# Two gate tiles moved behind the recurrence, two ahead of the sparse attention; the last expert pair summed in PSUM with the norm by halves

## Chip, cores and metric

The kernel runs on one core of a Trainium2 chip. The metric is the device time of one execution in microseconds (us). A core has TensorE (PE: matmuls, with its weight loads as PEld), VectorE (DVE), ScalarE (ACT), GpSimd (POOL) and SyncE (SP, which here issues most DMAs), each with its own instruction queue that is worked off in order. Engines wait for each other through semaphores.

## What is computed

Two blocks on 512 tokens of width 1024, all in float32. The first block has a recurrent branch, a sparse attention branch, two gates that mix them, and a mixture of 32 experts; its output goes through two norms into two layers of a second block. The lines that the change touches, cut from the reference:

```
xr, gr, q, ckv, qi, ki, wi, mg = jnp.split(u @ w_in[l], split_pts, axis=-1)
hr = rg_lru(causal_dwconv(xr, ...), ...)                       # recurrence, 1280 wide
y_a = (jax.nn.gelu(gr) * hr) @ w_rnn_out[l]
att = dsa_attention(q, rmsnorm(ckv, ...), qi, ki, wi, ...)     # top-128 keys of each query, 8 heads
y_b = att @ w_att_out[l]
ga, gb = jnp.split(jax.nn.sigmoid(mg), 2, axis=-1)             # two gates, 1024 wide each
mix = (ga * y_a + gb * y_b) @ w_out[l]
...
h = h + g2 * hier_moe(u2, ...)                                 # 32 experts, two per token
return rmsnorm(h, final_g)
# second block:
x = layer_norm(x, ln_in_g, ln_in_b)
for l in range(2): proj = x @ w_in[l]; ...
```

## The kernel before

A float32 product is made of three faster ones: each operand is split into a high part (`wh`, a cast on ScalarE, line 145) and a low part (`wl`, a subtraction on VectorE, line 146), and `mm3`/`mmk` (lines 300, 301, 303) add high times low, low times high and high times high in PSUM. So each weight piece costs ScalarE a cast, VectorE a subtraction, and TensorE three matmuls for each 128 rows. `FM.tile` makes one tile of 128 features by 512 tokens in this way: for an input of 1024 features 24 matmuls of 128x512, named `fm`. `TM` is the same with tokens in the rows; its `prepare` loads and splits the first pieces ahead of their use.

The kernel is written with a tile framework, which turns the program into one fixed queue of instructions for each engine. `weave` runs several generators beside each other and steps each in proportion to the weight given with it, so the weights set how their instructions interleave; `behind(a, b)` puts instruction a after b in that order without a semaphore.

`gate(d)` (line 677) makes one of 16 gate tiles: `fma.tile`, a sigmoid on ScalarE, a store to `gate_d` in HBM. Gates 0 to 7 are read again by `branch_a`, 8 to 15 by `branch_b`. In `rg_lru` (line 758) the recurrence goes through five groups of two blocks of 128 channels: `rg_first` (convolution), a gate tile, and, a group later, `rg_last` (the scan `hs`, a gelu gate `g2`, and its split `gT`). The group loop has a sixth pass that only runs the two last `rg_last`. Gates 0 to 9 are made there. It is woven with the index scores and the top-k selection (lines 638 and 639: maxima and replacements on VectorE). `branch_a` (line 784) then multiplies all ten `gT` with `w_rnn_out`, eight tiles of 30 matmuls.

In the sparse attention `att_score` (line 920) makes, for head h and query block i, the scores `as`, adds a bias (`bm`) and does a softmax (maximum `mx`, a sigmoid on ScalarE, reciprocal `su`); before head 0 it makes keys and values (`ak`, `av`) and the query tile of head 0, and at i = 3 the query tile of the next head. `att_out` transposes (`apt`) and splits (`pt`), `att_products` multiplies with the values (`ao`). It is woven, by `weave` on line 968, with `gate_b` (gates 10 to 15, weight 6) and `mod_rows` (vector-matrix products on VectorE, `macc`, with a short matmul `mrow`).

The experts run as 16 pairs. `pair_out` (line 1428) transposes the hidden rows (`hdt`, copied to `hp`), multiplies with the second weight (`e2`, both halves m of 512 columns in turns), and `outputs` (line 1297) scales to `y`, splits it (`yh`, `yl`), and `combine` adds the rows to the tokens: for each 128 tokens i and half m two matmuls with a 0/1 matrix `place` into PSUM (`cmb`), then a VectorE add to `h1[i][m]`. During one pair the `combine` of the pair before runs beside it. After the last pair (j = 15) the generator is emptied, then the loop at line 1964 norms each of four token tiles: squares on ScalarE with a sum (`ssq`), multiply by `final_g`, batch-norm statistics, and `norm` (line 1237), which ends in two halves of line 1240 and `turn`, the transposes `xt` and their splits `xT`. They feed `nav`, the first product of the second block, whose first three weight pieces are prepared (`nav_tm.prepare`) when the last pair is issued.

Of the kernel before, what the change touches and what calls it, by code (L numbers as in the profile page):

```python
# [64 lines left out]
def build(ctx, tc, I, out, dbg=None):  # L65
# [78 lines left out]
    def split(hi, lo, src, eng=None):  # L144
        S.copy(hi, src)  # L145
        (eng or V).tensor_tensor(lo, src, f(hi), OP.subtract)  # L146
# [234 lines left out]
    class TM:  # L381
# [25 lines left out]
        def piece(self, p, page=None):  # L407
# [7 lines left out]
            split(hi, lo, raw[:, k1:k1 + g1, :])  # L415
            return k0 + k1, g1, hi, lo

        def prepare(self):
            if self.first is None:
                self.first = [self.piece(p) for p in self.pieces[:self.lead]]  # L420
            return self
# [333 lines left out]
    def rg_lru():  # L755
        prev = []
        for g in range(6):
# [12 lines left out]
            if g < 5:  # L770
                prev = rg_decay(keep)
                yield

# [4 lines left out]
    weave((rg_lru(), 36), (chain(index_scores(), top_k(0, 6)), 44))  # L778
# [103 lines left out]
    def gate_b():  # L882
        for d in range(10, 16):
# [84 lines left out]
    weave((pipelined(8, att_score, att_out), 36), (gate_b(), 6), (mod_rows(0, 2, 1), 15))  # L968
# [262 lines left out]
    def normalizer(gvec, bvec, dst, paged=True):  # L1231
# [5 lines left out]
        def norm(i, v, mv, var, later=None):  # L1237
            r = rsqrt(var, 1, lambda: V.scalar_tensor_tensor(v, v, mv[:, 0:1], gR, OP.subtract, OP.mult))
            for cs in (slice(0, 512), slice(512, 1024)):
                V.scalar_tensor_tensor(v[:, cs], v[:, cs], r, bR[:, cs], OP.mult, OP.add)  # L1240
# [6 lines left out]
            else:  # L1247
                later.append(lambda: turn(i, v))

# [47 lines left out]
    def outputs(py, gtc, rows):  # L1297
# [12 lines left out]
        def combine():  # L1310
            after = yield
            for i in range(4):
                for m in range(2):
                    cs = slice(m * 512, m * 512 + 512)
                    ps = trp("cmb")
                    pl = place[:, i * 128:(i + 1) * 128]
                    mm = PE.matmul(ps, pl, yl[:, cs], start=True, stop=False)
                    if after is not None:
                        behind(mm, after)
                    PE.matmul(ps, pl, yh[:, cs], start=False, stop=True)  # L1320
# [108 lines left out]
    def pair_out(j, hd, ws):  # L1429
# [5 lines left out]
        S.copy(hp, b)  # L1435
        py = [mmp("e2") for _ in range(2)]
        for k in range(4):
            for m in range(2):
                cs = slice(m * 512, m * 512 + 512)
                both(py[m], hp[:, k * 128:k * 128 + 128], [w[:, cs] for w in ws[2 * k:2 * k + 2]], k == 0, k == 3)  # L1440
        return outputs(py, gt0[:, j:j + 1], rows0[:, :, j])
# [39 lines left out]
    for j in range(17):  # L1481
# [7 lines left out]
        if prev is not None:  # L1489
# [8 lines left out]
            if j == 16:  # L1498
                nav_tm.prepare()
        prev = hd  # L1500
    for _ in beside:
        pass
# [462 lines left out]
    for i in range(4):  # L1965
        a = h1t[i]

        ms = sm("ssq", 1)
        sq = pt_("sq", F32, (128, 1024))
        S.activation(sq, a, AF.Square, accum_out=ms)  # L1970
# [39 lines left out]
```

## Time and profile before

| | us |
|---|---|
| median of 3 runs | 3058.28 (3057.55 to 3060.16) |
| profiled execution | 3058.93, span 3057.2 |
| PE busy | 2893.9 (95%) |
| DVE busy | 1832.8 (60%) |
| ACT busy | 1137.3 (37%) |
| POOL busy | 196.3 (6%) |

Busy shares are means over stages with different limits. The mean granted TensorE clock is 0.987 of full speed. In the timeline rows a start time is in us from the start of the span, followed by the duration, and in brackets the idle time ahead of the instruction and what ended it. Instructions of one engine overlap a little, so the time from start to start is shorter than the duration shown.

### The profile page before, as it was taken

What the parts mean: (1) busy time and instruction counts of PE and PEld (TensorE: products, weight loads), DVE (VectorE), ACT (ScalarE), POOL (GpSimd) and SP (SyncE); (2) the same over time, 40 slices, a digit from 0 to 9 for tenths busy, and PEclk for the clock granted to TensorE, in tenths of its full rate; (3) what the DMA queues carried; (4) which work ended last, traced back from release to release, by engine and by line L of the source; (5) the groups of instructions that cost most, each with busy time, mean ns of one, the idle gap of its engine ahead of it and who ended that gap; (6) DMA issues with size and microseconds to landing.
All of it is one profiled execution on the core that took longest, in us unless ns stands there. A gap on an engine that the chain in (4) does not pass through costs nothing.

```text
span 3057.2 us, 36511 instructions
## 1 busy us (share of the span) xinstructions
PE 2893.9 (95%) x13749; PEld 2181.7 (71%) x13749; DVE 1832.8 (60%) x3549; ACT 1137.3 (37%) x1996; POOL 196.3 (6%) x216
## 2 busy tenths in 40 slices
PE   6999999889999979999999999999999989999998
PEld 5877777634333338888767888887888867788887
DVE  6899798733333265555888644436554689754434
ACT  4665244201000124444666322223443567332221
POOL 2000000100000001110002000000211000200000
PEclk9999999989999999999999999999999999999999
DMA  7333647789999964332335432424342234632342
GB/s 229 95 104 106 222 145 261 273 328 410 411 409 409 411 238 148 111 111 85 102 92 183 169 101 94 140 97 123 126 131 90 75 109 117 232 104 97 97 145 62
DMA packets 291648, 534.17 MB, mean 175 GB/s; under 512 B 29766, under 2 KB 172276, under 8 KB 287366
## 3 DMA queue, kind: packets, MB, share of 16 engines
q1 hardware_dynamic: 288872, 527.45, 49.4%
q0 software_dynamic: 2304, 4.20, 0.4%
q8 instruction: 110, 1.80, 0.3%
q14 instruction: 76, 0.62, 0.1%
q10 hardware_dynamic: 286, 0.09, 0.0%
HBM read 486.50 MB, written 44.38 MB: 174 GB/s over the span
## 4 chain that ended last, share of the span: by engine, by line
PE 56%; DMA 11%; DVE 6%; issue 3%; ACT 2%; POOL 1%; SPq 0%; DVEq 0%; POOLq 0%; ACTq 0%
PE fm L303 9%; PE fm L300 9%; PE fm L301 9%; DMA w<-in_moe_w_dram 7%; PE e L1391 4%; DMA w2r<-in_moe_w_dram 3%; PE ffo L303 2%; PE ffo L300 2%; PE ffo L301 2%; PE mix L300 1%; PE mix L301 1%; PE mix L303 1%; POOL tl L1666 1%; DVE wl L146 1%; DMA tl<-t_d 1%
## 5 line engine op out<-in xcount | busy, mean ns | idle before, releaser
L146 DVE TENSOR_TENSOR wl<-raw,wh 128x1024 fp32r<-128x1024 f32 (+3 forms) x403 | 461.7, 1147 | 307.9 <-ACT wh L145 306.3
L145 ACT CAST wh<-raw 128x1024 fp32r<-128x1024 f32 (+3 forms) x403 | 388.5, 966 | 550.0 <-PE fm L303 244.6
L300 PE MATMUL fm<-xT,wh 128*128 128x512 f32 (+1 forms) x1264 | 481.7, 384 | 0.0
L301 PE MATMUL fm<-xT,wl 128*128 128x512 f32 (+1 forms) x1264 | 479.5, 382 | 1.3 <-DVE wl L146 1.3
L303 PE MATMUL fm<-xT,wh 128*128 128x512 f32 (+1 forms) x1264 | 301.9, 381 | 0.0
L301 PEld LDWEIGHTS fm<-xT,wl 128*128 128x128 f32 x1264 | 238.3, 189 | 46.5 <-DVE wl L146 1.7
L300 PEld LDWEIGHTS fm<-xT,wh 128*128 128x128 f32 x1264 | 238.1, 188 | 45.0
L1391 PE MATMUL e<-w,xx 128*64 128x512 f32 x1024 | 257.1, 601 | 10.4 <-DMA w<-in_moe_w_dram 10.4
L303 PEld LDWEIGHTS fm<-xT,wh 128*128 128x128 f32 x1264 | 231.7, 188 | 45.5
L1391 PEld LDWEIGHTS e<-w,xx 128*64 128x64 f32 x1024 | 75.0, 137 | 157.7 <-issue 131.2
L1321 DVE TENSOR_TENSOR h<-h,cmb 128x512 f32<-128x512 f32 x128 | 80.7, 683 | 126.4 <-PE cmb L1320 126.2
L301 PE MATMUL fm<-uT,wl 128*128 128x512 f32 (+1 forms) x360 | 141.8, 394 | 2.7 <-DVE wl L146 2.6
L300 PE MATMUL fm<-uT,wh 128*128 128x512 f32 (+1 forms) x360 | 141.5, 395 | 0.0
L300 PE MATMUL ffo<-wl,hid 128*128 128x512 f32 x352 | 137.1, 390 | 0.0
L301 PE MATMUL ffo<-wh,hid 128*128 128x512 f32 x352 | 136.9, 389 | 0.0
L1391 PE MATMUL e<-w2r,hp 128*64 128x512 f32 x512 | 115.1, 596 | 10.1 <-ACT hp L1435 10.1
L1953 DVE SCALAR_TENSOR_TENSOR ffs<-ffs,fm 128x512 f32<-128x512 f32 x44 | 30.3, 688 | 137.7 <-ACT ffs L1952 137.7
L303 PE MATMUL ffo<-wh,hid 128*128 128x512 f32 x352 | 108.4, 389 | 0.0
L1955 DVE SCALAR_TENSOR_TENSOR ffs<-ffs,fm 128x512 f32<-128x512 f32 x44 | 30.2, 687 | 114.4 <-PE fm L303 114.4
L1952 ACT ACTIVATE ffs<-fm 128x512 f32<-128x512 f32 x44 | 26.3, 598 | 187.2 <-PE fm L303 187.2
L1391 PEld LDWEIGHTS e<-w2r,hp 128*64 128x64 f32 x512 | 41.1, 136 | 73.1 <-issue 58.3
L1307 DVE SCALAR_TENSOR_TENSOR y<-e,gts,g2R 128x512 f32<-128x512 f32 x32 | 22.9, 748 | 116.3 <-PE e L1391 116.0
(602 smaller groups left out, 5869.0 us busy)
## 6 DMA issues: line engine op xcount, KB each, us to landing
w<-in_moe_w_dram SPq DMA_DIRECT2D x192, 512.0 KB
raw<-in_w_in_dram SPq DMA_DIRECT2D x71, 1024.0 KB
w2r<-in_moe_w_dram SPq DMA_DIRECT2D x128, 512.0 KB
raw<-in_w_ffn_in_dram SPq DMA_DIRECT2D x44, 1024.0 KB
w<-in_moe_w_dram SPq DMA_DIRECT2D x32, 1024.0 KB
raw<-in_w_mod_dram SPq DMA_DIRECT2D x42, 512.0 KB
raw<-in_w_ffn_out_dram SPq DMA_DIRECT2D x20, 1024.0 KB
raw<-in_w_out_dram SPq DMA_DIRECT2D x12, 1024.0 KB
```

Of the source, the lines that this page charges most:

```text
L145: S.copy(hi, src)
L146: (eng or V).tensor_tensor(lo, src, f(hi), OP.subtract)
L300: PE.matmul(ps, l[0], r[1], start=start and n == 0, stop=False)
L301: PE.matmul(ps, l[1], r[0], start=False, stop=False)
L303: PE.matmul(ps, l[0], r[0], start=False, stop=stop and n == len(pairs) - 1)
L1307: V.scalar_tensor_tensor(y[:, cs], py[m], gtc, g2R[:, cs], OP.mult, OP.mult)
L1321: V.tensor_tensor(h1[i][m], h1[i][m], ps, OP.add)
L1391: mm = PE.matmul(ps[hs], lhs[:, hs], rhs[h], start=start, stop=stop)
L1666: G.tensor_tensor(th, m, th, OP.add)
L1952: S.activation(s, pgt, AF.Tanh, scale=0.5)
L1953: V.scalar_tensor_tensor(s, s, 1.0, pgt, OP.add, OP.mult)
L1955: V.scalar_tensor_tensor(s, s, 0.5, pup, OP.mult, OP.mult)
```

## The change

It has two parts. In the first, gates 10 and 11 are made at the end of `rg_lru`, after the last two `rg_last` (and the weave weight goes from 36 to 38); gates 12 and 13 are made ahead of the attention weave, and only 14 and 15 stay in it, with weight 2. In the second, for the last pair the products of `e2` run half by half, the table of the reciprocal square root is loaded on ScalarE right behind the copy `hp`, and the old rows `h1` are added by a matmul with the identity that opens each PSUM group, so `combine` hands over the PSUM tile and the VectorE add goes. The norm's squares and its multiply by `final_g` read that tile, half by half, in the order `LAST`; the statistics come by halves too. `nav_tm.prepare` runs inside the norm of token tile 0, its splits behind that tile's last operation.

```diff
         def prepare(self, after=None):
             if self.first is None:
-                self.first = [self.piece(p) for p in self.pieces[:self.lead]]
+                self.first = []
+                for p in self.pieces[:self.lead]:
+                    self.first.append(self.piece(p))
+                    if after is not None:
+                        behind(self.low, after)
...
             if g < 5:
                 prev = rg_decay(keep)
                 yield
+            else:
+                for d in (10, 11):
+                    gate(d)
+                    yield
...
-    weave((rg_lru(), 36), (chain(index_scores(), top_k(0, 6)), 44))
+    weave((rg_lru(), 38), (chain(index_scores(), top_k(0, 6)), 44))
...
     def gate_b():
-        for d in range(10, 16):
+        for d in range(12, 16):
...
-    weave((pipelined(8, att_score, att_out), 36), (gate_b(), 6), (mod_rows(0, 2, 1), 15))
+    gb = gate_b()
+    for _ in range(2):
+        next(gb)
+    weave((pipelined(8, att_score, att_out), 36), (gb, 2), (mod_rows(0, 2, 1), 15))
...
+    BANKS = [(i, m) for i in range(4) for m in range(2)]
+    LAST = [(0, 0), (1, 0), (0, 1), (1, 1)] + BANKS[4:]
...
         def combine():
             after = yield
-            for i in range(4):
-                for m in range(2):
+            for i, m in LAST if last else BANKS:
+                cs = slice(m * 512, m * 512 + 512)
+                ps = trp("cmb")
+                pl = place[:, i * 128:(i + 1) * 128]
+                if last:
+
+                    PE.matmul(ps, ident, h1[i][m], start=True, stop=False)
+                mm = PE.matmul(ps, pl, yl[:, cs], start=not last, stop=False)
...
+                PE.matmul(ps, pl, yh[:, cs], start=False, stop=True)
+                if last:
+                    after = yield ps
+                else:
                     V.tensor_tensor(h1[i][m], h1[i][m], ps, OP.add)
                     after = yield
...
+        steps = [(k, m) for k in range(4) for m in range(2)]
+        if j == 15:
+
+            steps.sort(key=lambda e: (e[1], e[0]))
+            behind(S.activation(const("table", [128, 1]), ones[:, 0:1], AF.Abs_reciprocal_sqrt), cast)
...
+    def norm_parts(i, m, ps):
+        a = h1[i][m]
+        if m == 0:
+            sts[i] = sm("ssq", 2), sm("bst", 12)
+        S.activation(sqs[i % 2][:, m * 512:m * 512 + 512], ps, AF.Square, accum_out=sts[i][0][:, m:m + 1])
+        V.tensor_tensor(a, ps, fgR[:, m * 512:m * 512 + 512], OP.mult)
+        bn_part(a, sts[i][1], m, 2)
+
+    def norm_in(i):
+        ms, st = sts[i]
+        v = sm("msq", 1)
+        V.tensor_scalar(v, ms[:, 0:1], ms[:, 1:2], 1e-6 * 1024, OP.add, OP.add)
+        mv = bn_done(st)
+        V.scalar_tensor_tensor(v, v, 1e-5 / 1024, mv[:, 1:2], OP.mult, OP.add)
+        return norm(i, h1t[i], mv, v)
+
+    sqs = [pt_("sq", F32, (128, 1024)) for _ in range(2)]
+    for n, (i, m) in enumerate(LAST):
+        norm_parts(i, m, beside.send(None))
+        if m:
+            last = norm_in(i)
+            if i == 0:
+                nav_tm.prepare(last)
...
-    for i in range(4):
-        a = h1t[i]
...
-        norm(i, a, mv, v)
```

How this moves instructions on the engines shows in three places. VectorE at the end of the recurrence, before (`g` and `gT` of the last two blocks, `m` and `selp` the top-k):

```order
429 L749 SCALAR_TENSOR_TENSOR g_442_2388<-g_442_2388,fm_2359 128x512
430 L747 SCALAR_TENSOR_TENSOR g_449_2435<-g_449_2435,fm_2406 128x512
431 L750 TENSOR_TENSOR g_442_2388<-g_442_2388,hs_2355 128x512
432 L639 MATCH_REPLACE selp_735<-m_459_2493,selp_735 128x256
433 L749 SCALAR_TENSOR_TENSOR g_449_2435<-g_449_2435,fm_2406 128x512
434 L146 TENSOR_TENSOR gT_2394<-g_442_2388,gT_2394 128x512
```

and now:

```order
428 L751 SCALAR_TENSOR_TENSOR g_447_2429<-g_447_2429,fm_2400 128x512
429 L754 TENSOR_TENSOR g_440_2382<-g_440_2382,hs_2349 128x512
430 L146 TENSOR_TENSOR wl_2480<-raw_2441,wh_2479 128x1024
431 L146 TENSOR_TENSOR gT_2388<-g_440_2382,gT_2388 128x512
432 L753 SCALAR_TENSOR_TENSOR g_447_2429<-g_447_2429,fm_2400 128x512
433 L146 TENSOR_TENSOR wl_2520<-raw_2514,wh_2519 128x640
```

The split `wl_2480` of gate 11 stands between the `g` of the last but one block and its `gT`; the two 128x640 splits of `branch_a`, which stood further ahead, come behind it. On TensorE at the same place, gate 11 is `fm_2478` and the first tile of `branch_a` is `fm_2518`; now:

```order
1115 L303 MATMUL fm_2443<-uT_398,wh_2444 128x512
1116 L300 MATMUL fm_2478<-uT_226,wh_2479 128x512
1117 L300 MATMUL fm_2518<-gT_1174,wh_2519 128x512
1118 L301 MATMUL fm_2478<-uT_226,wl_2480 128x512
1119 L300 MATMUL fm_2478<-uT_236,wh_2479 128x512
```

Before, `branch_a` began in row 1092, right behind the last tile of the recurrence; now gate 10 (`fm_2443`) and gate 11 stand between. TensorE at the scores of head 0, query block 3 (`as` with 128x512), before:

```order
1449 L303 MATMUL fm_3201<-uT_398,wh_3202 128x512
1450 L300 MATMUL as_3233<-kP_3034,qT_3110 128x512
1451 L301 MATMUL as_3233<-kP_3034,qT_3110 128x512
1452 L303 MATMUL as_3233<-kP_3034,qT_3110 128x512
1453 L300 MATMUL fm_3321<-uT_226,wh_3322 128x512
1454 L301 MATMUL fm_3321<-uT_226,wl_3323 128x512
```

and now:

```order
1545 L303 MATMUL fm_3333<-uT_398,wh_3334 128x512
1546 L300 MATMUL as_3365<-kP_3166,qT_3242 128x512
1547 L301 MATMUL as_3365<-kP_3166,qT_3242 128x512
1548 L303 MATMUL as_3365<-kP_3166,qT_3242 128x512
1549 L300 MATMUL as_3378<-kP_3176,qT_3362 128x128
1550 L959 MATMUL apt_3392<-ident,bm_3249 128x128 x2
```

Before, a gate tile (`fm_3321`, gate 11) and the query tile of head 2 followed these scores; now the first scores of head 1 and the transposes of head 0 follow at once, and gates 12 and 13 stand ahead of the keys instead. VectorE at the norms, from the end of token tile 1 to the first multiply of token tile 2, before:

```order
1563 L1240 SCALAR_TENSOR_TENSOR h_962_4959<-h_962_4959,rst_9674,lnb_9517 128x512 x2
1564 L146 TENSOR_TENSOR xT_9630<-xt_9645,xT_9630 128x128
1565 L1971 TENSOR_TENSOR h_963_4962<-h_963_4962,fgR_9513 128x1024
1566 L146 TENSOR_TENSOR xT_9631<-xt_9645,xT_9631 128x128
1567 L146 TENSOR_TENSOR xT_9624<-xt_9680,xT_9624 128x128
```

and now:

```order
1561 L1251 SCALAR_TENSOR_TENSOR h_962_4959<-h_962_4959,rst_9664,lnb_9517 128x512 x2
1562 L146 TENSOR_TENSOR xT_9602<-xt_9670,xT_9602 128x128
1563 L146 TENSOR_TENSOR xT_9603<-xt_9670,xT_9603 128x128
1564 L146 TENSOR_TENSOR xT_9606<-xt_9683,xT_9606 128x128
1565 L146 TENSOR_TENSOR xT_9604<-xt_9670,xT_9604 128x128
1566 L146 TENSOR_TENSOR xT_9607<-xt_9683,xT_9607 128x128
1567 L146 TENSOR_TENSOR xT_9605<-xt_9670,xT_9605 128x128
1568 L1530 TENSOR_TENSOR h_963_4962<-cmb_9697,fgR_9513 128x512
```

Six `xT` splits of the tile just finished stand ahead of the next tile's multiply, which stood ahead of them.

## Rows read from the trace of the kernel before

**Rows 1.** Windows: stretch, length; busy PE, PEld, DVE, ACT, POOL; clock, DMA share, GB/s.

```profile
260.00:280.00 20.00, 18.52 (x82) 14.91 (x80) 20.00 (x33) 15.76 (x24) 0.00 (x0) 1.00 0.15 47
282.00:290.00 8.00, 5.30 (x13) 3.77 (x14) 6.84 (x18) 1.97 (x4) 0.00 (x0) 0.57 0.53 149
386.00:496.00 110.00, 109.33 (x568) 87.76 (x567) 105.46 (x241) 53.96 (x120) 0.00 (x0) 0.99 0.51 174
380.00:500.00 120.00, 116.97 (x590) 92.27 (x590) 113.86 (x258) 58.77 (x129) 0.00 (x0) 0.97 0.50 169
1110.00:1147.00 37.00, 23.56 (x93) 15.76 (x91) 35.93 (x82) 14.75 (x40) 1.40 (x2) 0.82 0.22 80
```

**Rows 2.** Timeline of PE, `branch_a`: start, us, instruction, [idle before, what ended it].

```profile
273.34 0.39 PE L300 MATMUL fm<-gT,wh 128*128 128x512 f32 x1
...
278.83 0.50 PE L301 MATMUL fm<-gT,wl 128*128 128x512 f32 x1 [1.48 <-DVE wl L146]
...
283.67 0.79 PE L300 MATMUL fm<-gT,wh 128*128 128x512 f32 x1 [3.40 <-DVE gT L146]
...
285.92 0.80 PE L300 MATMUL fm<-gT,wh 128*128 128x512 f32 x1 [1.03 <-DVE gT L146]
...
336.64 0.27 PE L180 MATMUL rowst<-ident,rows 60*128 60x60 f32 x1
```

**Rows 3.** Timeline of DVE at the end of the recurrence.

```profile
263.54 1.22 DVE L146 TENSOR_TENSOR wl<-raw,wh 128x1024 fp32r<-128x1024 f32 x1
...
277.95 0.82 DVE L146 TENSOR_TENSOR wl<-raw,wh 128x640 fp32r<-128x640 f32 x1
278.69 1.22 DVE L743 TENSOR_TENSOR_SCAN hs<-ra,tx 128x512 f32<-128x512 f32 x1
...
281.33 0.69 DVE L750 TENSOR_TENSOR g<-g,hs 128x512 f32<-128x512 f32 x1
```

**Rows 4.** Waits of PE from 200 to 260: total, times, longest.

```profile
PE fm L301 <- DVE wl L146: 2.6, 3, 1.2
```

**Rows 5.** Timeline of PE, front of the attention (queries, gate 10, scores).

```profile
342.58 0.40 PE L300 MATMUL fm<-uT,wh 128*128 128x512 f32 x1
...
348.05 0.39 PE L300 MATMUL fm<-uT,wh 128*128 128x512 f32 x1
...
350.94 0.33 PE L301 MATMUL as<-kP,qT 128*128 128x128 f32 x1 [1.21 <-DVE nlam L866]
...
361.74 0.39 PE L300 MATMUL as<-kP,qT 128*128 128x512 f32 x1
```

**Rows 6.** Timeline of DVE, start of the softmax chain to the first `pt`.

```profile
367.98 0.29 DVE L860 TENSOR_TENSOR lp<-lv 128x128 f32<-128x128 f32 x1 [4.67 <-DMA lv<-in_diff_lambda_dram]
...
380.42 1.28 DVE L806 SCALAR_TENSOR_TENSOR macc<-raw,csil,macc 128x1024 f32<-128x1024 f32 x1
...
381.69 0.67 DVE L146 TENSOR_TENSOR pt<-apt,pt 128x512 fp32r<-128x512 f32 x1
```

**Rows 7.** Timeline of PE, last pair and norm.

```profile
1099.61 7.09 PE L1391 MATMUL e<-w2r,hp 128*64 128x512 f32 x32 [0.68 <-ACT hp L1435]
1108.15 0.50 PE L1317 MATMUL cmb<-yl,place 128*128 128x512 f32 x1 [1.45 <-DVE yl L146]
...
1124.10 1.97 PE L1257 MATMUL xt<-ident,h 128*128 128x128 f32 x8 [11.06 <-DVE h L1240]
```

**Rows 8.** One tile's instructions, `mrow`: durations in ns, first and last start.

```profile
L814 PE MATMUL mrow<-macc,ones x4: 590/592/592, 401.2 to 402.5; 128*1 128x512 f32 x4
```

**Rows 9.** Timeline of DVE, last adds, `nav` splits, first and last norm end.

```profile
1109.77 3.67 DVE L1321 TENSOR_TENSOR h<-h,cmb 128x512 f32<-128x512 f32 x6 [0.15 <-PE cmb L1320]
1113.36 2.35 DVE L146 TENSOR_TENSOR wl<-raw,wh 128x1024 fp32r<-128x1024 f32 x2
...
1123.30 1.41 DVE L1240 SCALAR_TENSOR_TENSOR h<-h,rst,lnb 128x512 f32<-128x512 f32 x2
...
1145.58 1.42 DVE L1240 SCALAR_TENSOR_TENSOR h<-h,rst,lnb 128x512 f32<-128x512 f32 x2
```

## Prediction before the run

> **What bounds the kernel now.** I read the page's busy shares first (TensorE fills the span, so only places where it waits or repeats work can move the end), then the windows, timelines and waits of the three stretches that the diff touches, and the chain of waits behind them. The first two stretches stand ahead of the experts' weight stream, which is released by the router and hence by what lies before it; the third stands behind it. So a gain or loss in each is carried to the end one for one.
>
> At the end of the recurrence VectorE has no gap: 20.00 of 20 us in 260 to 280 [rows 1]. TensorE is ahead of it: `branch_a` starts at 273.34, then waits 1.48, 3.40 and 1.03 us for the splits `wl`, `gT` and `gT`, and ends at 336.64 [rows 2]. Behind the long wait the granted clock is 0.57 of full speed in 282 to 290, a mean over the 1.2 and 2.4 GHz levels; TensorE is busy 5.30 us there with 13 matmuls [rows 1], which at 0.227 us apart (as ahead of the wait) take 2.95: some 2.1 to 2.3 us lost to the clock. The hole is thus 5.9 of waits and about 2.1 of slow clock.
>
> In the sparse attention both engines are nearly full: 386 to 496 has TensorE at 109.33 and VectorE at 105.46 of 110 us; 380 to 500 leaves VectorE 6.14 us idle [rows 1]. The start of the softmax chain is what the front has to reach: VectorE waits 4.67 us for the load `lv`, begins at 367.98, and splits the first `pt` at 381.69 [rows 6].
>
> In the last stretch VectorE is the bound: eight adds of the last pair, three splits of `nav` weights, then four norms; 35.93 busy of 37 us [rows 1, 9], while TensorE stands 11.06 us until the first `xt` [rows 7].
>
> **Part A1, gates 10 and 11 behind the recurrence.** One gate tile or query tile of 24 matmuls takes 5.47 us (342.58 to 348.05) [rows 5]; two bring 10.94 us of TensorE work ahead of `branch_a`, into a hole of 8.0. Filling all of it would cost 2.9 us. But the second gate needs its own `wl`, which is a VectorE operation of 1.22 us in the stream that is already full [rows 1, 3]. In the new order it stands behind `g2` times `hs` of the last but one block, which starts at 281.33 and frees VectorE at 281.93 [rows 3]. Up to there the new order has one `wl` of 1024 more (+1.13 issue to issue), two `wl` of 640 fewer (-0.74 each, the next starting at 278.69 after 277.95) and one top-k maximum fewer (about -0.4): VectorE arrives at 281.2, and `wl` is ready at 282.4. TensorE arrives sooner: VectorE has some 1.7 us less top-k work in front at the time of the first gate, and TensorE's 2.6 us of waits on `wl` between 200 and 260 [rows 4] can shrink by that, so gate 10 runs 271.6 to 277.1 and gate 11 stops after its first matmul and one of `branch_a`, at 277.4. It waits 5 us where before there was work, then has 23 matmuls (5.2) and 239 of `branch_a` (54.3) to go: 341.9 against 336.64, **+5.2**. The clock would be low behind that wait as it is now behind the 3.40 (2.1 lost), so I take **+7.3** for the end of `branch_a` (E). Ends: clock loss 0 to 3.4 (all of 282 to 289 at half speed), VectorE's lead 0.8 better or worse: +4.4 to +9.4. The `gT` splits, later by one `wl`, are covered by gate 11. Queued behind the new waits: on ScalarE the table load and gate 10's sigmoid stand ahead of the last `g2` tanh and both `gT` casts, which VectorE does not want before 283; on SP's queue the two gate stores stand ahead of a `w_rnn` load that is read two tiles, over 13 us, later. Both cost nothing unless the second gate ends after about 295.
>
> The Trainium skill, in "Perfetto Trace Analysis", section Optimization Strategies, says to keep the matmul engine as highly used as possible, and where it waits, to relieve the engines that block the path. The first half speaks for this move, the second against it, since the blocking engine gets two splits more; by the first alone A1 is the 2.9 of a filled hole (below as a rival), by the rows it is 7.3.
>
> **Part A2, gates 12 and 13 ahead of the attention, 10 and 11 gone from it.** Before, the front from E runs: keys and values to 342.58 (5.9), `q0` 5.47, then a gate mixed with scores and `q1` to 361.74 (13.7, of it 1.21 a wait for a small VectorE chain that now lies earlier) [rows 5]. The four scores of head 0 ended at E+25.8 and the chain then waited for `lv`, E+31.3. Now two gates (10.9) precede: 10.9 + 5.9 + 5.5 + 12.5 + 0.7 = E+35.5, plus 0.6 for `bm`: the chain starts at E+36.1, the load is long there. From its start to the first `pt` it took 13.7 us [rows 6]; in the new order one `macc` of 1.28 [rows 6] stands behind instead: 12.4, so first `pt` at E+48.5 against E+45.05 (381.69 less 336.64): **+3.4**. After that TensorE has 10.9 us less to do, but VectorE's work to the last `att` shrinks by only 0.9 (two `wl` of a query or gate tile go, one `macc` comes). VectorE can win at most its 6.14 us of idle. TensorE is the fuller of the two, so some of that idle is its doing; the waits left are latencies of the chain from score to transpose to split, which no lighter TensorE removes. I take 3.7 of the 6.1: 3.4 - 0.9 - 3.7 = **-1.2**. Ends: nothing recovered +2.5, all of it -3.6.
>
> **Part B, last pair and norm.** Removed on VectorE: eight adds of 0.60 us issue to issue (six in 3.67) [rows 9], 4.8 us. Three `wl` (3.4, two in 2.35 [rows 9]) move from ahead of norm 0 to behind it. Added on TensorE: eight identity matmuls in plain fp32; the nearest row is `mrow`, where two such products are four records from 401.2 to 402.5 [rows 8], 0.43 apart, so 0.86 each: 6.9 us, the first beside the wait for `hp`'s result, the rest in TensorE's 11.06 us [rows 7] or between transposes while VectorE works; if that cover is gone, up to 0.86 a half. The first half of the pair's output comes some 3 us sooner, as its products are half of 7.09 [rows 7], and the table load leaves ScalarE's path. Working norm 0 through: the second `y` at 1107.6 (0.86 + 7.09 behind 1099.61), both halves in PSUM by 1110.9, multiply, statistics, the four small steps and two halves of the end: 1116.1 instead of 1124.71 (1123.30 + 1.41 [rows 9]): -8.6. Then the three `wl` go back in ahead of norm 1 (-3.4), and the new order puts six of the eight `xT` splits of a tile ahead of the next tile's first multiply, where before that multiply (1.2) and the statistics filled the time until transpose and cast were there. Before, tiles took 7.4 us (1123.30 to 1145.58 is three [rows 9]) without a gap; I give norm 1 9.7 and the next two 9.1 each, 1.7 for transposes (eight took 1.97 at the low clock [rows 7]) and first cast on the path. Norm 3 ends at 1144.0 instead of 1147.0 (1145.58 + 1.42): **-3.0**. Ends: the adds and all idle of the stretch (37 less 35.93 [rows 1]) saved, -5.9; ten us for each of the last two tiles, -1.2.
>
> **Sum:** 7.3 - 1.2 - 3.0 = +3.1. The profiled execution took 3058.93 us, which is 3062.0; the median of the runs lies 0.65 lower, so **3061.4**.
>
> **Rivals.** *Slower:* VectorE sets both A stages. Then lighter TensorE gives the attention nothing, the late chain start stays (+2.5), `branch_a` is late with all the slow clock (+9.4), and transposes hold the norms (-1.2): +10.7, 3069. For it: 20.00 of 20, and a late chain. Against: TensorE at 109.33 of 110. It passes the bound once `wl` of gate 11 comes later than 282 and under 1.5 us of attention idle is won back. *Faster:* TensorE sets both A stages, as the utilisation figures would have it. The hole is filled (+2.9), attention gives its idle back (-3.6) and about 1 us of slow clock at 386 to 396, norms -5.9: -7.6, 3050.7. It needs `wl` at 277.5, five us before VectorE is there by the rows. The sentence of the skill quoted above would give this one. *Not what it says:* B gains its bound of 5.9 while A comes out as forecast (+6.1): +0.2, 3058.5, within the bound too.
>
> **Numbers.** Within 0.2% (6.1 us, about what a measurement of this kernel can tell from no change) lie the forecast and the last rival, 0.49 together; the slower rival and its neighbourhood above 3064.4 get 0.33, the faster one 0.18. The range runs from the faster rival to the slower one, 3050.5 to 3069.
>
> **What would show it.** A1: in the new profile a TensorE wait of about 5 us on `wl` near 277, clock low behind it, `branch_a` ending near 344; wrong if that wait is under 2 us. A2: first `pt` at E+48; VectorE idle in the 120 us behind it about 2.5 instead of 6.1; last `att` about 1 us nearer to E. B: norm 0 ending 8.6 us sooner against the pair's `hp`, then 9 us tiles with VectorE waits on `xT` casts. The forecast fails most easily if the attention turns out to be set by TensorE after all, or if the tiles of the norm do not stretch.

## The result, and the profile after

The changed kernel takes 3079.48 us (median of 6 runs, 3077.44 to 3081.04), the kernel before 3059.22 (6 runs, 3057.39 to 3063.15). The ratio is 1.0065 with a 95% interval of 1.0053 to 1.0077: slower, by 20.3 us, where +3.1 was forecast and the range ended at 3069.

The page of the changed kernel, its span and its busy times:

```profile
span 3078.1 us, 36562 instructions
PE 2906.1 (94%) x13765; PEld 2190.2 (71%) x13765; DVE 1832.8 (60%) x3545; ACT 1139.0 (37%) x2005; POOL 197.6 (6%) x216
```

TensorE's share hardly moved, so the places have to be read one by one. Five landmarks stand in both programs: E (the first product behind `branch_a`), the first `mix` product behind the attention's output, the last pair's copy `hp`, the first `fm` product behind `nav`, and the end.

| stretch | before | after | difference | forecast |
|---|---|---|---|---|
| start to E | 336.64 | 344.04 | +7.4 | +7.3 |
| E to `mix` | 208.87 | 217.78 | +8.9 | -1.2 |
| `mix` to `hp` | 553.46 | 553.92 | +0.5 | 0 |
| `hp` to first `fm` | 58.39 | 59.18 | +0.8 | -3.0 |
| first `fm` to the end | 1899.84 | 1903.18 | +3.3 | 0 |
| sum (span) | 3057.2 | 3078.1 | +20.9 | +3.1 |

**End of the recurrence**, timeline of PE, columns as in [rows 2]; the first row is the second gate's first product:

```profile
276.82 0.39 PE L300 MATMUL fm<-uT,wh 128*128 128x512 f32 x1
280.02 0.80 PE L300 MATMUL fm<-gT,wh 128*128 128x512 f32 x1 [2.81 <-ACT ga L684]
282.87 0.80 PE L301 MATMUL fm<-uT,wl 128*128 128x512 f32 x1 [2.05 <-DVE wl L146]
...
344.04 0.27 PE L180 MATMUL rowst<-ident,rows 60*128 60x60 f32 x1
```

What the second gate waits for, timeline of DVE, which answers to [rows 3]:

```profile
281.59 1.22 DVE L146 TENSOR_TENSOR wl<-raw,wh 128x1024 fp32r<-128x1024 f32 x1
```

The gate issues one product and stops; one of `branch_a` is squeezed in when ScalarE is done with `ga`, the sigmoid of gate 10, and the next of the gate comes when `wl` is there. E itself varies by some us between executions: the programs that are the same up to E end there at 335.83 to 339.06 without the two gates, and at 344.04 to 346.04 with them.

**The attention.** Windows, columns as in [rows 1]. Of the kernel before, from E to `mix`:

```profile
336.64:545.51 208.87, 198.96 (x962) 157.60 (x962) 177.64 (x387) 87.94 (x168) 2.01 (x3) 0.98 0.62 212
```

Of the changed kernel, the stretch behind the second gate's wait, two stretches inside the attention, and the whole from E to `mix`:

```profile
280.00:290.00 10.00, 7.93 (x26) 6.05 (x26) 10.00 (x21) 2.44 (x5) 0.00 (x0) 0.69 0.35 118
...
384.00:394.00 10.00, 3.40 (x13) 2.68 (x13) 10.00 (x35) 3.81 (x11) 0.00 (x0) 0.56 0.31 100
...
504.00:514.00 10.00, 5.98 (x18) 2.96 (x19) 9.91 (x21) 2.37 (x6) 0.00 (x0) 0.70 0.46 113
...
344.04:561.82 217.78, 195.10 (x915) 151.31 (x915) 176.35 (x383) 83.63 (x163) 2.01 (x3) 0.95 0.57 192
```

TensorE's idle time is the length less its busy time: 9.91 us before, 22.68 after. The granted clock (the column before DMA) fell from 0.98 to 0.95. The trace's record of the clock puts 10.24 us of the stretch at the lower level (1.2 GHz) before and 23.89 after; half of it is the clock loss as it is counted here, 5.1 and 12.0. Busy time less that loss is the work at full clock: 193.8 and 183.2. So two gates, 10.7 us, did leave the stretch, but idle time grew by 12.8 and the clock took 6.8: -10.7 + 12.8 + 6.8 = +8.9. The clock's part is an upper bound, since for 3.2 us of the low level before and 7.4 after TensorE stood idle; over its busy time alone the loss is 3.5 and 8.3, and the sum reads -8.6 + 12.8 + 4.8. VectorE's busy time is the same (177.64, 176.35).

What TensorE waits for there, the longest sums, before (total, times, longest):

```profile
PE apt L951 <- DVE mx L940: 2.8, 2, 1.6
PE mrow L814 <- DVE macc L806: 1.9, 2, 1.4
PE as L301 <- DVE qT L146: 1.7, 1, 1.7
PE ao L300 <- DVE pt L146: 1.2, 1, 1.2
```

and after:

```profile
PE as L300 <- ACT qT L145: 7.5, 1, 7.5
PE ao L300 <- DVE mx L948: 3.3, 4, 1.3
PE apt L959 <- DVE bm L952: 3.3, 2, 1.8
PE apt L959 <- DVE bm L945: 2.3, 3, 1.8
PE mrow L822 <- DVE macc L814: 1.8, 1, 1.8
```

One wait stands out, 7.5 us ahead of the second query head's scores (`as`). Timelines of PE, ScalarE and VectorE there, the place of [rows 5] and [rows 6]. TensorE:

```profile
379.94 0.39 PE L303 MATMUL as<-kP,qT 128*128 128x512 f32 x1
387.87 0.47 PE L300 MATMUL as<-kP,qT 128*128 128x128 f32 x1 [7.54 <-ACT qT L145]
```

ScalarE:

```profile
371.85 0.57 ACT L145 CAST qT<-fm 128x512 fp32r<-128x512 f32 x1
```

The line above is of the kernel before, the query tile of head 1; the changed kernel:

```profile
386.64 0.61 ACT L950 ACTIVATE bm<-bm,mx 128x384 f32<-128x384 f32 x1 [1.71 <-DVE mx L948]
387.16 0.19 ACT L950 ACTIVATION_READ_ACCUMULATOR bm<-bm,mx 128x1 f32 x1
387.25 0.56 ACT L145 CAST qT<-fm 128x512 fp32r<-128x512 f32 x1
```

VectorE of the changed kernel:

```profile
380.37 0.69 DVE L945 SCALAR_TENSOR_TENSOR bm<-as,bm 128x512 f32<-128x512 f32 x1 [5.60 <-PE as L303]
...
393.36 0.68 DVE L146 TENSOR_TENSOR pt<-apt,pt 128x512 fp32r<-128x512 f32 x1
```

The query's products had all been issued before 379.94, but its cast `qT` stands on ScalarE's queue behind a sigmoid of head 0, and that waits for VectorE's `mx`. Before, the cast came as late, 10.1 us behind the start of the fourth score at 361.74 [rows 5] (now 7.8 behind 379.49), but there a gate and a query tile (48 products, 10.9 us) stood between the fourth score of head 0 and these scores, and TensorE did not wait for it. Now there is nothing. The order rows shown with the change say so: `as` follows `as` where a gate (`fm`) stood.

**The norm.** Timeline of DVE, ends of the four norms and what stands between the second and the third (of before [rows 9]):

```profile
1132.01 1.41 DVE L1251 SCALAR_TENSOR_TENSOR h<-h,rst,lnb 128x512 f32<-128x512 f32 x2
...
1141.86 1.41 DVE L1251 SCALAR_TENSOR_TENSOR h<-h,rst,lnb 128x512 f32<-128x512 f32 x2
1143.65 0.29 DVE L146 TENSOR_TENSOR xT<-xt,xT 128x128 fp32r<-128x128 f32 x1 [0.39 <-ACT xT L145]
1144.28 1.54 DVE L146 TENSOR_TENSOR xT<-xt,xT 128x128 fp32r<-128x128 f32 x5 [0.33 <-ACT xT L145]
1146.12 0.69 DVE L1530 TENSOR_TENSOR h<-cmb,fgR 128x512 f32<-128x512 f32 x1 [0.30 <-ACT sq L1529]
...
1148.28 0.69 DVE L1530 TENSOR_TENSOR h<-cmb,fgR 128x512 f32<-128x512 f32 x1 [0.49 <-ACT sq L1529]
...
1151.83 1.41 DVE L1251 SCALAR_TENSOR_TENSOR h<-h,rst,lnb 128x512 f32<-128x512 f32 x2
...
1161.79 1.42 DVE L1251 SCALAR_TENSOR_TENSOR h<-h,rst,lnb 128x512 f32<-128x512 f32 x2
```

Counted from `hp` (1098.97 before, 1115.74 after), the end of norm 0 begins at +16.27 instead of +24.33, 8.1 us sooner. Then a tile takes 9.85, 9.97 and 9.96 us instead of 7.4 on the mean, and norm 3 is only 0.56 sooner. VectorE had been full there; now, in the same 37 us ahead of norm 3's end, it is busy for 32.35.

### The profile page after: what moved, and what is told of

It is laid out like the page before. It is cut to its first block, busy times and chain, and to the rows that moved or that the text cites. A ratio compares the mean times of both kernels' runs of the same rounds, so it can differ in the third digit from the quotient of the medians.

```text
span 3078.1 us, 36562 instructions
## 1 busy us (share of the span) xinstructions
PE 2906.1 (94%) x13765; PEld 2190.2 (71%) x13765; DVE 1832.8 (60%) x3545; ACT 1139.0 (37%) x2005; POOL 197.6 (6%) x216
## 4 chain that ended last, share of the span: by engine, by line
PE 58%; DMA 9%; DVE 5%; issue 3%; ACT 2%; POOL 1%; SPq 0%; DVEq 0%; POOLq 0%; ACTq 0%
PE fm L300 9%; PE fm L303 9%; PE fm L301 9%; DMA w<-in_moe_w_dram 6%; PE e L1411 6%; DMA w2r<-in_moe_w_dram 3%; PE ffo L301 3%; PE ffo L300 3%; PE ffo L303 3%; POOL tl L1711 1%; PE mix L300 1%; PE mix L301 1%; PE mix L303 1%; PE cmb L1334 1%; DVE wl L146 1%
```

## The experiments

The theories at the start: *one*, the softmax chain's late start costs the attention; *two*, a gate in the weave is cover: TensorE works on it while softmax steps of other engines are under way, and without it it waits and its clock falls; and against both, that TensorE's work, or VectorE's, sets the stage.

**Only the gates, and only the norm.** The change's two parts, each alone, with the text as in the change.

> Only the gates are moved (10 and 11 behind the recurrence, 12 and 13 ahead of the attention); last pair and norm as before. In the changed kernel the last attention tile is split 16.3 us later than before and the last pair's copy hp stands 16.8 us later, 0.8 more is there at the first product behind nav. If the gates are the whole loss, this kernel is 16 to 19 us slower than the kernel before (3075 to 3078), with branch_a ending near 344, the first pt near 393.4 and the last att near 521. If the last pair and norm carry a good part, it is under 14 us slower.

> Only the last pair and the norm are changed. Theory one (each norm tile takes 10 us instead of 7.4 because VectorE waits for ScalarE casts and squares, which eats the 8 us that tile 0 wins): norm 3 ends 0 to 1 us sooner against hp, first product behind nav 0 to 1 us later: the time within 1.5 us of the kernel before. Theory two, my prediction: 3 us faster. If the 2 to 3 us that the changed kernel loses behind the norm belong to this part, it is 3 us slower.

Gates only: 3079.47 us, ratio 1.0061 (1.0044 to 1.0077). Norm only: 3061.69, ratio 1.0003 (0.9993 to 1.0013), `hp` to first `fm` 57.53, so 0.9 us won. The whole loss is the gates', and the norm part is worth nothing that can be measured.

**The two halves of the gate part.** Two gates behind the recurrence and four in the weave; or two ahead of the attention and four in the weave:

```diff
+                for d in (10, 11):
+                    gate(d)
+                    yield
...
-    weave((pipelined(8, att_score, att_out), 36), (gate_b(), 6), (mod_rows(0, 2, 1), 15))
+    weave((pipelined(8, att_score, att_out), 36), (gate_b(), 4), (mod_rows(0, 2, 1), 15))
```

```diff
-    weave((pipelined(8, att_score, att_out), 36), (gate_b(), 6), (mod_rows(0, 2, 1), 15))
+    gb = gate_b()
+    for _ in range(2):
+        next(gb)
+    weave((pipelined(8, att_score, att_out), 36), (gb, 4), (mod_rows(0, 2, 1), 15))
```

> Gates 10 and 11 behind the recurrence, none ahead of the attention, 12 to 15 woven in with weight 4. The front of the attention on TensorE is as before (keys, values, queries, one gate among the first scores). Theory one (the late start of the softmax chain is what costs): branch_a ends 7.4 us later, first pt at 45 us behind it as before, and from there to the last att 121 to 123.4: 5.5 to 7.5 us slower than before in all. Theory two (a gate taken out of the weave leaves TensorE waiting and at half clock): the stretch from first pt to last att grows by about half of the changed kernel's 4.6: 9 to 11 us slower.

> Gates 10 and 11 ahead of the attention, 12 to 15 woven in with weight 4, none behind the recurrence. branch_a ends as before (336.6). Theory one: the first pt comes 4.3 us later (49.3 behind branch_a), and from there to the last att 123.4 as before: 4 to 5 us slower. Theory two: that stretch grows by about 2.3 as well: 6 to 8 us slower. If instead TensorE set this stage, two gates more ahead and two fewer inside would cancel: within 1 us of the kernel before.

Behind only: 3071.5 us, ratio 1.0034 (1.0022 to 1.0046; the seven runs spread from 3065.22 to 3076.48); E at 344.12, first `pt` at E+45.20, so no later than before, and still E to `mix` takes 213.96 instead of 208.87 with 10.8 us less work. But the stretch where theory two put the loss, from the first `pt` to the last `att`, took 122.68 us, as theory one said; the loss lies behind the last `att`, 46.08 us to `mix` instead of 40.47. There TensorE had more left to do: 16 of the 192 products of `branch_b` (those on `att`) were issued ahead of the last `att`, before 30. Ahead only: 3076.37, ratio 1.0053 (1.0036 to 1.0069; the profiled execution is the shortest of the four, 3070.01), so 16 us slower, where the theories had 4 to 8; E at 337.04, first `pt` at E+49.34, from there to the last `att` 129.24 instead of 123.35, where theory two had 2.3 more; E to `mix` 221.24 with the work of before. Neither half is harmless, and neither theory does by itself. The second half, with as much work as before, shows that place matters, not amount.

**One gate behind the recurrence, five in the weave; and eight in the weave** (gates 8 and 9 taken from the recurrence).

```diff
+                for d in (10,):
+                    gate(d)
+                    yield
...
-    weave((pipelined(8, att_score, att_out), 36), (gate_b(), 6), (mod_rows(0, 2, 1), 15))
+    weave((pipelined(8, att_score, att_out), 36), (gate_b(), 5), (mod_rows(0, 2, 1), 15))
```

```diff
-                    gate(2 * g + n)
+                    if g < 4:
+                        gate(2 * g + n)
...
-        for d in range(10, 16):
+        for d in range(8, 16):
```

> Gate 10 alone behind the recurrence, gates 11 to 15 in the weave with the attention, nothing ahead of it. The recurrence's end: TensorE needs no new `wl` there, so its waits of 5.9 us ahead of `branch_a` should be filled and the end of `branch_a` (336.6 before) moves by 0 to +2. Theory one (gates in the weave are cover for waits on the softmax chain): the stretch from the end of `branch_a` to the first `mix` product, 208.9 before, 213.96 with two gates out, comes to 211 to 212 with one out, though TensorE has 5.4 less to do; in all 3061 to 3065. Theory two (TensorE's work sets the stretch and the two-gate run was a clock accident): 203 to 206, in all 3053 to 3057.

> The other way round: gates 8 and 9 go from the recurrence into the weave, so that eight gates lie beside the attention. TensorE gets 10.9 us more there and 10.9 less in the recurrence. Cover theory: from the end of `branch_a` to the first `mix` product 208.9 grows by 0 to 5, since waits and half clock shrink; what the recurrence gives back is 3 to 9 us if VectorE's stream sets its end (two `wl` of 1.2 leave it), in all 3050 to 3059. Theory of TensorE setting the attention: the stretch grows by the full 10.9, and the recurrence, set by VectorE, gives back 2.5 only: 3066 to 3068.

One behind: 3066.48 us, ratio 1.0026 (1.0015 to 1.0037); E at 337.42, E to `mix` 212.34, nearly the 211 to 212 of the cover theory (the whole is 1.5 us above its range). The hole at the recurrence's end holds one gate for 0.8 us, which is within the spread of E, and not two. Eight in: 3076.44, ratio 1.0058 (1.0044 to 1.0072); E 2.1 us sooner, but E to `mix` 221.76, 12.9 more for 10.3 us more of work. Here the expectation of the cover theory (0 to 5 more) was wrong: beyond six, a gate covers nothing, and its whole work is added.

**Gates made again for nothing.** As "behind only", but gates 10 and 11 are computed a second time in the weave at their old places. The result isn't needed; the order of TensorE's products in the attention is that of before.

```diff
+    def again():
+        for d in (10, 11):
+            gate(d)
+            yield
...
-    weave((pipelined(8, att_score, att_out), 36), (gate_b(), 4), (mod_rows(0, 2, 1), 15))
+    weave((pipelined(8, att_score, att_out), 36), (chain(again(), gate_b()), 6), (mod_rows(0, 2, 1), 15))
```

> Gates 10 and 11 behind the recurrence as in the run of that half alone, and made a second time in the weave beside the attention, at their old places: 10.9 us of TensorE work and some VectorE splits that nobody needs, with TensorE's order in the attention that of the kernel before. Cover theory: from the end of `branch_a` to the first `mix` product it falls from 213.96 back to 208.5 to 209.5, as before, and the whole is 4 to 6 us shorter than with two gates out although it does 10.9 us more: end of `branch_a` 344, in all 3065 to 3068. Theory of TensorE's work setting the stage: 213.96 and 5 to 11 more, in all 3076 to 3083.

It takes 3066.95 us, ratio 1.0019 (1.0010 to 1.0028), against 3071.5 and 1.0034 for "behind only"; the two intervals overlap a little. Windows from E to `mix` and from the last `att` to `mix`, first without, then with the useless gates:

```profile
344.12:558.08 213.96, 193.31 (x914) 150.17 (x914) 177.11 (x385) 83.54 (x163) 2.02 (x3) 0.95 0.60 200
512.00:558.08 46.08, 43.88 (x182) 33.34 (x181) 35.93 (x39) 15.34 (x14) 2.02 (x3) 0.96 0.81 270
```

```profile
345.09:552.73 207.64, 198.58 (x962) 157.31 (x962) 177.67 (x388) 86.44 (x167) 2.02 (x3) 0.98 0.62 213
512.24:552.73 40.49, 39.02 (x168) 30.61 (x167) 34.90 (x39) 14.95 (x14) 2.02 (x3) 1.00 0.81 287
```

48 more products, and the stretch is 6.3 us shorter, with the granted clock back at 0.98. Up to the last `att` it is nearly the same, 167.15 us for 167.88: there the useless gates cost nothing. The other 5.6 us lie behind it, where 14 products fewer are left (3.2 us at 0.227 each) and the clock loss is 0 instead of 1.7. So the run shows that these two gates are free in the weave. How much of the 6.3 us is cover for waits, and how much the order of `branch_b`'s products, which changes with the weave, it doesn't separate. TensorE's waits from E to `mix`, first without (the two on `qT`), then with:

```profile
PE as L300 <- ACT qT L145: 4.3, 1, 4.3
PE as L301 <- DVE qT L146: 3.1, 3, 1.5
```

```profile
PE as L301 <- DVE qT L146: 2.0, 2, 1.7
```

All kernels of the gate part, in us (work, idle and clock loss from E to `mix`, the loss as counted first above; `qT` is the sum of TensorE's waits on it):

| gates behind / ahead / in the weave | E | E to last `att` | E to `mix` | work | idle | clock loss | `qT` |
|---|---|---|---|---|---|---|---|
| before: 0 / 0 / 6 | 336.64 | 168.40 | 208.87 | 193.8 | 9.9 | 5.1 | 1.7 |
| 2 / 0 / 6, two of them again | 345.09 | 167.15 | 207.64 | 193.5 | 9.1 | 5.1 | 2.0 |
| 0 / 0 / 8 | 334.52 | 176.89 | 221.76 | 204.2 | 12.5 | 5.1 | 1.7 |
| 1 / 0 / 5 | 337.42 | 170.16 | 212.34 | 189.2 | 18.0 | 5.1 | 7.7 |
| 2 / 0 / 4 | 344.12 | 167.88 | 213.96 | 183.1 | 20.7 | 10.2 | 7.4 |
| 0 / 2 / 4 | 337.04 | 178.58 | 221.24 | 194.3 | 18.4 | 8.5 | 8.1 |
| 2 / 2 / 2 (gates only) | 346.04 | 177.78 | 218.09 | 181.4 | 23.1 | 13.7 | 7.8 |
| 2 / 2 / 2 (changed kernel) | 344.04 | 177.32 | 217.78 | 183.2 | 22.7 | 12.0 | 7.9 |

Wherever fewer than six gates lie in the weave, `qT` is waited for some 6 us longer. With four or five in it the even spread puts the second gate behind the query tile of head 2, so that 24 products instead of 48 stand between the two heads' scores; with two ahead, none.

Read down to the last `att`, the table takes the change apart. From before to "behind only" (two gates fewer in the weave) it is 0.5 us less; from there to "ahead only" (two gates put ahead) 10.7 more; from there to the changed kernel (two fewer again) 1.3 less; together the change's +8.9. So two gates ahead cost nearly their whole 10.9 us, and four gates taken out of the weave, 21.9 us of work, gave back 1.8. Up to `mix` the same steps are +5.1, +7.3 and -3.5: taking two gates out cost 5.1 in one place and paid 3.5 in the other, so neither is a price per gate. Each step rests on one profile of each kernel, and equal programs differ by up to 1.1 us in these stretches.

**The norm's tiles.** In the first kernel the Square goes behind the multiply of the same half; in the second, besides, the transposes and splits of a tile are issued behind the next tile's multiplies and statistics:

```diff
-        S.activation(sqs[i % 2][:, m * 512:m * 512 + 512], ps, AF.Square, accum_out=sts[i][0][:, m:m + 1])
         V.tensor_tensor(a, ps, fgR[:, m * 512:m * 512 + 512], OP.mult)
+        S.activation(sqs[i % 2][:, m * 512:m * 512 + 512], ps, AF.Square, accum_out=sts[i][0][:, m:m + 1])
```

```diff
-        return norm(i, h1t[i], mv, v)
+        return norm(i, h1t[i], mv, v, later)
...
         if m:
+            while later:
+                later.pop(0)()
             last = norm_in(i)
```

> The pair and norm change alone, with the Square issued behind the multiply of the same half, and nothing else moved. Theory P: the waits of 0.3 to 0.5 us of VectorE's statistics and multiplies on the Square go, tiles fall from 9.97 to about 9.0, 54 to 55 us from `hp` to the first product behind `nav`. Theory C: tiles stay at 9.6 to 10, 57 to 58; in all as the change alone, 3060 to 3062.

> The pair and norm change alone, with two differences: VectorE's multiply stands ahead of ScalarE's Square on each half, and the transposes and splits of a tile are issued behind the next tile's multiplies and statistics. Theory C (the tiles of 9.97 us come from the splits `xT` standing ahead of the next tile's first multiply, waiting for transposes and casts): tiles fall to 7.4 to 8, and from `hp` to the first product behind `nav` it is 51 to 54 instead of 57.5 (norm change alone) and 58.4 (before); in all 3053 to 3056. Theory P (ScalarE's Square and VectorE's multiply on one PSUM tile hold each other up): tiles stay at 9 or above, 56 to 58, in all 3058 to 3061.

Square behind: 3059.83 us, ratio 0.9996 (0.9987 to 1.0006); tiles of 9.62, 9.90 and 11.55, `hp` to first `fm` 58.23. Turn deferred: 3057.7, ratio 0.9991 (0.9982 to 1.0); `hp` to first `fm` 52.97 (the 53.65 in the expectations of the two runs below is three products too late). Its tiles take 8.52, 9.00 and 5.79 us, 7.8 on the mean, and the whole is 1.7 us above the 3053 to 3056 expected. Theory C holds in the main: the tiles stretch since a tile's splits stand ahead of the next tile's multiplies. Theory P falls: with the Square moved, the first two tiles are those of the norm part alone (9.62, 9.95). Of the deferred kernel, VectorE's waits from the first norm's end to the last norm's:

```profile
DVE xT L146 <- ACT xT L145: 0.8, 2, 0.6
```

In the changed kernel, the same stretch:

```profile
DVE h L1530 <- ACT sq L1529: 1.7, 5, 0.5
DVE xT L146 <- ACT xT L145: 1.4, 4, 0.4
```

The kernel with only the Square moved trades the wait on `sq` for one on the sums: 2.9 us on `cmb`, whose products stand on TensorE's queue behind transposes that wait for the norm before.

**Once more, and row by row.** The deferred kernel again, and with the last sums taken tile by tile:

```diff
-    LAST = [(0, 0), (1, 0), (0, 1), (1, 1)] + BANKS[4:]
+    LAST = BANKS
```

> The deferred variant once more, for a second profile of the same program: from `hp` to the first product behind `nav` 53.6 again. From there to the end, where the program is that of the kernel before, the first profile took 1903.9 us with 18.6 of clock loss, before 1899.8 with 13.6. If that is tied to the change, 18 to 19 again; if it falls out anew in every execution, anything from 13 to 19. In all 3054 to 3061.

> The deferred variant of the pair and norm change, with the sums of the last pair taken tile by tile instead of the first halves of two tiles first. If VectorE's order sets norm 0 there, its multiply and statistics of tile 1's first half (1.25 us) go behind norm 0, the first transposes come 1.0 to 1.3 us sooner and the first product behind `nav` 0.5 to 1.3 (53.65 to 52.4 to 53.1); if norm 0 waits for the second half of the pair's output anyway, 53.6 to 54.0. In all 3055 to 3058.

Again: 3056.64 us, ratio 0.9986 (0.9977 to 0.9995), `hp` to first `fm` 52.97 once more. Row by row: 3056.62, ratio 0.9987 (0.9978 to 0.9996), 52.46. Both beat the kernel before, by 0.13 to 0.14%. The step from one to the other is 0.5 us where 0.5 to 1.3 was expected, and can't be measured in the whole.

## Why the prediction was wrong

**What bounds the kernel: right as a reading, wrong in what it was used for.** TensorE at 109.33 of 110 us [rows 1] was read as a sign that less work for TensorE shortens the stage, or does nothing. The fill was there because gates lay between the steps of the softmax chain: of four gates taken out of it, 21.9 us, 1.8 came back up to the last `att`.

**A1: right, with its parts.** E came at 344.04 for 343.9. A wait of about 5 us near 277 was forecast; there are two, 2.81 and 2.05, with one product between, which waited for the sigmoid of gate 10. `wl` was to be ready at 282.4; it began at 281.59 and took 1.22. The clock was low for 6.8 us there, as long as before. The run with one gate fits (0.8 us for one, 7.5 for two), but doesn't separate `wl` from the size of the hole: one gate's 5.5 us fit into its 8.0, two gates' 10.9 do not. That E came within 0.1 us is luck: equal programs spread over 2 us.

**A2: the step that failed is "VectorE can win at most its 6.14 us of idle ... I take 3.7 of the 6.1".** The first term was nearly right where it was read: `pt` at E+49.32, +4.3 for +3.4. But from there to `mix` -0.9 and -3.7 were put down, and +4.6 came (163.82 to 168.46); the last `att`, forecast 1 us nearer to E, came 8.9 later. Two things were wrong. The credit: two gates fewer in the weave brought back 0.5 and 1.3 us up to the last `att`, where 4.6 were put down. And the price of the two gates ahead doesn't end at the first `pt`: it is 10.7 us at the last `att`. Work had moved past that landmark: the query tile of head 2 is cast at E+62.0 instead of E+37.6, so its 24 products come behind the first `pt`. The text named the reason for the first itself ("latencies of the chain from score to transpose to split") and drew half of it: a lighter TensorE doesn't shorten such a latency. The other half is that a TensorE without other work in that time stands, and that its clock was low there (0.56 in 384 to 394), where products start 0.43 us apart instead of 0.227. VectorE's idle time from the first `pt` to the last `att`, which was to shrink from 6.1 to 2.5, is 12.89 in 128.0 us, against 8.67 in 123.35. The useless gates show the credit to be near nothing: with 10.4 us more work (193.5 for 183.1) the way to the last `att` was no longer, and the way to `mix` 6.3 us shorter. The ends of the term were wrong too: "nothing recovered" (+2.5) was no bound, since "behind only" lost 5.1 us with a chain that began no later.

The chain of the largest single wait is read from the trace: query tile, its cast behind a sigmoid on ScalarE's queue, that behind `mx` of VectorE. VectorE is full there (10.00 of 10 us in 384 to 394), and that `mx` stands in its queue behind a `macc` of 1.28. Neither order was tried by itself, by an earlier cast or a later `macc`; that the wait comes and goes with the products between is shown by the table. Nor is this wait the bulk: up to the first `att` TensorE stood 10.8 us, before 7.6. The other 9.6 of the 12.8 us come later, in waits of up to 1.8 us on VectorE, and what makes them is open. With one gate behind, 3.5 us were lost at an unchanged clock loss: idle time grew by 8.1 for 4.6 of work less.

The Trainium skill, in "Perfetto Trace Analysis", section Optimization Strategy, says that where the most contended engine changes over time, interleaving such regimes may help. The change undid such an interleaving, and this is the rule that should have been a rival: the traces agree in part, with +5.1 us up to `mix` for the first two gates taken out of the weave, but -3.5 for the next two and 12.9 for two more than six, and the rule does not say how much is enough.

**The rivals.** The slower one had the sign, and both its conditions came (`wl` at 282.8, no idle time won back), but not the cause: the amount of VectorE's work doesn't set the attention, since the useless gates raise it from 177.11 to 177.67 us in a shorter stretch, though in places like 384 to 394 VectorE is full; and its late chain start, 2.5 us, was under a third of what came. The faster one asked for `wl` at 277.5, which came at 282.8. That the norm would gain 5.9 fell too.

**B: the mechanism was right, the sizes off.** Norm 0 was forecast 8.6 us sooner and is 8.1; the tiles were to be 9.7, 9.1 and 9.1 and are 9.85, 9.97 and 9.96, so of -3.0 only -0.56 is left at norm 3. The term that was mis-sized is the tiles, 27.9 us for three and measured 29.8. The forecast had the cast and transposes on the path but not ScalarE's Square, for which VectorE's multiply waits five times, 0.34 us on the mean; yet moving the Square won 0.0 and 0.05 us on the first two tiles, so what the other 1.9 us are stays open. The Trainium skill, in "PSUM — Partial Sum Buffer", section PSUM bank collisions raise a hardware error, says that the compiler makes any two engines that touch the same bank and quadrant of partitions take turns, reads too; the trace agrees (1.7 us in five waits with the Square ahead, and with the Square behind, ScalarE waits for the multiply instead). Alone, the part gives 0.9 us up to the first `fm`; in the changed kernel norm 3 ends 0.3 us later than that, and behind it to the first `fm` stand 13.13 us instead of 11.74, with a clock loss of 1.7 instead of none, so that nothing is left of it.

**The last 3.3 us** lie behind the first `fm`, where the program is the same. In the 13 profiles this stretch takes 1899.2 to 1904.9 us, and its clock loss is 13.6 to 18.9; length less loss is 1884.4 to 1887.1 in all of them. So the difference goes with the clock. Windows of the same place, before and in the changed kernel:

```profile
1732.40:1742.40 10.00, 9.90 (x82) 9.90 (x83) 3.64 (x11) 3.92 (x8) 0.00 (x0) 1.00 0.37 121
```

```profile
1750.00:1760.00 10.00, 9.47 (x56) 9.11 (x55) 4.24 (x11) 3.21 (x9) 0.00 (x0) 0.66 0.45 157
```

In the 10 us ahead TensorE is busy 7.63 us before and 8.16 after, so it waits in both; then the changed kernel loses 3.4 us to the clock, and the kernel before nothing. Why it falls in one execution and not in the other stays open: the deferred kernel's two profiles have 18.6 and 17.5 us of loss there, its row-by-row form 14.0, and before 13.6. With the norm part the loss tends to be higher (14.0 to 18.9, without it 13.6 to 16.9), but these overlap, and no run separates them. It can account for the deferred kernel, 5.4 us ahead at the first `fm`, being only 2.9 to 3.8 ahead in the whole.

## What to carry to other kernels

A busy engine in a stage of long chains may be busy with filler, and filler is worth what it covers: before moving it, list for each wait of the chain which product stands beside it now and which will after. Look for a cast that stands on another engine's queue behind a chain step; here it was the first to surface when the filler went. Price a move at the end of the stage, not at a landmark inside it, since work can move past the landmark: 4.3 us at the first `pt` were 10.7 at the last `att`. When an operation moves ahead in one tile, look at what it then stands in front of in the next: the norm gained 8 us at its start and lost them over three tiles until the turn was deferred.

## What was not expected of the hardware

- Useless work can be free: 48 more products left the way to the last `att` as long (167.15 us for 167.88), and the clock loss from E to `mix` fell from 10.2 us to 5.1. The stretch ended 6.3 us sooner, in part because other products stood in another order.
- The granted clock makes equal programs differ: in the same stretch of 1900 us, 13.6 to 18.9 us lost. The stretch's spread is 5.7 us, and 2.7 without that loss.
